# Up-projection with 512-column products on a joined activation tile, and an eviction in three stages

## The chip, the cores and the metric

The kernel runs on one core of one Trainium2 chip. The metric is the device time in microseconds of that core. Three runs of the kernel before took 1162.98, 1164.25 and 1164.31 us; their median is 1164.25 us. Engine names are those of the profile: PE is TensorE's matmul, PEld its weight load, DVE is VectorE, ACT is ScalarE, POOL is GpSimd, SP is SyncE.

## The reference

One layer of a decoder trunk on 256 tokens of width 2048: a mixing block (sparse attention beside a causal convolution) with its residual, then a gated MLP with a causal depthwise convolution of three taps, then a last norm. The change lies in the MLP, and there in the up-projection:

```python
def conv_glu_ffn(h, w_up, cw, cb, w_down):
    u = causal_depthwise_conv(h @ w_up, cw, cb)
    a, gate = jnp.split(u, 2, axis=-1)
    return (jax.nn.silu(gate) * a) @ w_down
...
    h = rms_norm(x, ffn_norm_g[l])
    x = x + conv_glu_ffn(h, w_up[l], ffn_conv_w[l], ffn_conv_b[l], w_down[l])
return rms_norm(x, final_norm_g)
```

`h` is 256 x 2048, `w_up` 2048 x 11264 (5632 columns for `a`, then 5632 for `gate`), `w_down` 5632 x 2048; all values are float32.

## The kernel before

**Numbers in two parts.** TensorE takes float32 operands here in the fp32r format, which keeps fewer bits. So each operand is held as a high part (the value rounded to fp32r) and a low part (what the rounding left). A product is made of three: high by high, high by low, low by high. `mm3` (L137 to L139) does this with the weights stationary: `wh` by `xt_h`, `wh` by `xt_l`, `wl` by `xt_h`, each 128 x 128 weights by 128 x 256 activations, added up in one PSUM bank. `mm_rows` (L144 to L146) does it with the activations stationary and 512 weight columns moving; the out-projection and the down-projection use it.

**Weights.** They come in chunks of 128 x 2048 floats (1 MB) in a fixed list, by DMA from SP's queue into one of three `wraw` buffers. `w_split` makes the high part on ScalarE (L109, `wh`) and the low part on VectorE (L114, `wl`, which needs `wh`); some chunks early in the kernel have their low part made on GpSimd. When the low part is done, the DMA of the chunk three places later is released. `w_next` hands chunk c to TensorE and, ahead of that, puts the split of chunk c + 2 into the queues of ScalarE and VectorE. There are three pairs of `wh` and `wl` buffers, so the high part of chunk c + 2 waits until TensorE has finished chunk c - 1.

**Order.** The schedule is manual: each engine does its instructions in the order in which the program issues them. The stages follow each other on TensorE: in-projection with attention and convolution woven in, out-projection, up-projection, down-projection, last norm.

**Up-projection.** The activations are transposed, in two tiles `xt_h` and `xt_l` of 128 x 16 x 256 (16 blocks of the contraction, 256 tokens); `norm_evac` (L177 on ScalarE, L178 on VectorE) fills them from the transposed residual. The norm's factor per token, `rB`, is not in them and is multiplied into the result. The loop has 22 rounds `m`, each with two passes `part` (0 for `a`, 1 for `gate`), each with two weight chunks `kh`. A pass makes two tiles of 128 features x 256 tokens, in the left halves of two PSUM banks, from 2 x 16 blocks of weights. The eight banks are used in turn by four passes. During the first pass the last transposes of the residual and the spreading of `rB` are put between the products (`between`).

After the products of a pass, its eviction is issued at once, one tile after the other. `conv3` multiplies the bank by `rB` into `u` on VectorE (L898), makes the third tap with its bias on ScalarE (`yt`, L900) and adds the other two taps on VectorE (L903 twice). In part 1, ScalarE then makes the silu (`sgf`, L935) and VectorE multiplies it with part 0's tile into `gt` (L936). All this stands in the queues of ScalarE and VectorE ahead of the next chunk's split.

**Down-projection.** `gsplit` splits four tiles of `gt` at a time into high and low (L892, L893), two groups ahead, eleven groups twice over. `down_chunk` then makes 512-column products into four banks.

Of the kernel before, what the change touches and what calls it, by code (L numbers as in the profile page):

```python
# [11 lines left out]
F32 = mybir.dt.float32  # L12
# [5 lines left out]
P = 128  # L18
# [28 lines left out]
def hybrid_trunk(ctx: ExitStack, tc: tile.TileContext, a: dict, out: bass.AP):  # L47
# [133 lines left out]
    x_rows = a["x"].rearrange("(t p) d -> p t d", p=P)  # L181

    mixp = ctx.enter_context(tc.tile_pool(name="mix", bufs=1))
    xt_h = mixp.tile([P, KD, T], F32R, name="xt_h")
    xt_l = mixp.tile([P, KD, T], F32R, name="xt_l")
    rB = mixp.tile([P, T], F32, name="rB")


# [683 lines left out]
    with ExitStack() as fx:  # L872
# [20 lines left out]
            nc.vector.tensor_sub(gl, src, gh.bitcast(F32))  # L893
            gq.append((gh, gl))

        def conv3(c, bank):
            u = fw.tile([P, T], F32, name="u", bufs=4)
            nc.vector.tensor_mul(u, bank[:, :T], rB)  # L898
            yt = fw.tile([P, T], F32, name="yt", bufs=6)
            nc.scalar.activation(yt, u, AF.Identity, scale=fcw[:, c, 2:3], bias=fcw[:, c, 3:4])  # L900
            for k in (1, 0):
                d = 2 - k
                nc.vector.scalar_tensor_tensor(yt[:, d:], u[:, :T - d], fcw[:, c, k:k + 1], yt[:, d:],  # L903
                                               op0=OP.mult, op1=OP.add)
            return yt


        for t in range(2):
# [5 lines left out]
        for m in range(NFT // 2):  # L914
            ya = {}
            if m == NFT // 2 - 1:
                gsplit()
            for part in range(2):
                bk = UP_BANKS[2 * ((2 * m + part) % 4):][:2]
                for kh in range(2):  # L920
                    wh, wl = [w.rearrange("p (k c) -> p k c", c=256) for w in w_next(1 if m + part + kh else 2)]
                    for n, (k, i) in enumerate((k, i) for k in range(8) for i in range(2)):
                        kt = kh * 8 + k
                        sl = slice(i * P, (i + 1) * P)
                        mm3(bk[i][:, :T], wh[:, k, sl], wl[:, k, sl], xt_h[:, kt], xt_l[:, kt],
                            kt == 0, kt == KD - 1)
                        if m + part == 0 and (kh, n) in between:
                            between.pop((kh, n))()
                for i in range(2):
                    yt = conv3(part * NFT + 2 * m + i, bk[i])  # L930
                    if part == 0:
                        ya[i] = yt
                    else:
                        sg = fw.tile([P, T], F32, name="sgf", bufs=2)
                        nc.scalar.activation(sg, yt, AF.Silu)  # L935
                        nc.vector.tensor_mul(gt[:, 2 * m + i], sg, ya[i])  # L936

        NQ = NFT // 4
        ss3 = fp.tile([P, 2, 5], F32, name="ss3")
# [43 lines left out]
        for h in range(2):  # L983
            prev, db = db, [(bank[2:] + bank[:2])[4 * h + 2 * t:][:2] for t in range(2)]
            for q in range(NQ):
                g = gq.pop(0)
                gsplit()
                if h == 1 and q == NQ - 1:
                    for t in range(2):
                        nc.vector.tensor_add(x2[:, t, 1536:], db[t][1], x2[:, t, 1536:])  # L990
                w0 = w_next()
                if prev and 0 < q < 5:
                    first_half(prev, (q - 1) // 2, (q - 1) % 2)
                if h == 1 and q == NQ - 1:
                    w1_ = w_next()
                    for t in range(2):
                        last_rows(w0, w1_, g, db[t], t)
                    break
                for t in range(2):
                    down_chunk(w0, g, db[t], 2 * q, t)  # L1000
                w1_ = w_next()
                for t in range(2):
                    down_chunk(w1_, g, db[t], 2 * q + 1, t)

# [87 lines left out]
```

## Time and profile before

| what | value |
|---|---|
| median of three runs | 1164.25 us |
| profiled execution: its own time | 1164.46 us |
| profiled execution: its span | 1162.7 us |
| PE, PEld, DVE, ACT busy, share of the span | 98%, 91%, 64%, 50% |
| mean granted TensorE clock | 0.993 |
| up-projection, first product to first product of the down-projection | 398.48 to 907.02 us |

A row of a group of instructions reads: line, engine, operation, written tile <- read tiles, sizes, count | busy us, mean ns of one | idle time of the engine just before them and what ended it. A row of the timeline reads: start in us from the span's start, duration in us, engine, line, operation. A row of the busy time in a stretch reads: the stretch, its length, then busy time of PE, PEld, DVE, ACT and POOL with the number of instructions, granted clock, DMA share, GB/s. Ends of matmuls are modelled and consecutive ones overlap, so a matmul's cost in a stream is the distance from one start to the next, not its duration. The weight load's row (PEld) lies beside the products.

### The profile page before, as it was taken

To read this page: it belongs to the slowest core of one execution; us is meant where nothing else is said; L and a number is where in the kernel's file an instruction comes from. 1 tells how busy PE (TensorE), PEld (TensorE's weight loads), DVE (VectorE), ACT (ScalarE), POOL (GpSimd) and SP (SyncE) were. 2 spreads that over 40 slices of the span, in tenths; PEclk is the share of its full clock that TensorE was granted. 3 is DMA by queue.
4 is the path that set the end of the run, shared out by engine and by line. 5 is a ranking of instruction groups with operands and counts; after the bars stand their busy time and mean duration, and the time that the engine had idled before them with its cause. 6 is when DMAs were issued, how large, how long until landed. Compare 5 with 4: busy or idle time off the path is not lost.

```text
span 1162.7 us, 18834 instructions
## 1 busy us (share of the span) xinstructions
PE 1136.0 (98%) x7890; PEld 1058.0 (91%) x7890; DVE 748.7 (64%) x1162; ACT 582.3 (50%) x810; POOL 128.2 (11%) x80
## 2 busy tenths in 40 slices
PE   8999999889899999999999999999999999999997
PEld 8999999888778899999999999999999888888886
DVE  6699569676455666667666666666666655556544
ACT  6534256788754544444535444544454444444443
POOL 1979553000000000000000000000000000000000
PEclk9999999999999999999999999999999999999998
DMA  9567416222264545545554545454545555555551
GB/s 367 194 240 260 152 53 252 73 79 94 70 265 152 211 169 194 204 160 183 181 215 147 198 174 209 145 215 171 196 149 210 191 182 203 185 185 181 182 180 73
DMA packets 32290, 207.62 MB, mean 179 GB/s; under 512 B 3867, under 2 KB 6187, under 8 KB 8012
## 3 DMA queue, kind: packets, MB, share of 16 engines
q1 hardware_dynamic: 28592, 199.64, 48.0%
q10 hardware_dynamic: 3612, 6.76, 1.6%
q8 instruction: 62, 1.02, 0.4%
q14 instruction: 24, 0.20, 0.1%
HBM read 204.27 MB, written 2.12 MB: 178 GB/s over the span
## 4 chain that ended last, share of the span: by engine, by line
PE 87%; ACT 5%; DVE 4%; DMA 2%; issue 1%; POOL 1%; DVEq 0%; POOLq 0%; ACTq 0%
PE bank L139 18%; PE bank L137 18%; PE bank L138 18%; PE bank L146 9%; PE bank L145 9%; PE bank L144 9%; DMA xr<-in_x 2%; ACT wh L109 1%; PE bank L437 1%; ACT e L643 1%; DVE wl L114 1%; PE bank L677 1%; ACT e L658 1%; PE bank L664 1%; POOL wl L114 0%
## 5 line engine op out<-in xcount | busy, mean ns | idle before, releaser
L137 PE MATMUL bank<-xt_h,wh 128*128 128x256 f32 x1920 | 546.9, 285 | 1.8 <-ACT wh L238 1.7
L139 PE MATMUL bank<-xt_h,wl 128*128 128x256 f32 x1920 | 544.8, 284 | 1.8 <-POOL wl L114 1.5
L138 PE MATMUL bank<-xt_l,wh 128*128 128x256 f32 x1920 | 544.5, 284 | 0.0
L114 DVE TENSOR_TENSOR wl<-wraw,wh 128x2048 fp32r<-128x2048 f32 (+1 forms) x185 | 360.6, 1967 | 126.9 <-ACT wh L109 126.8
L109 ACT ACTIVATE wh<-wraw 128x2048 fp32r<-128x2048 f32 (+2 forms) x239 | 352.7, 1501 | 135.7 <-PE bank L146 68.7
L137 PEld LDWEIGHTS bank<-xt_h,wh 128*128 128x128 f32 x1920 | 369.3, 192 | 3.9 <-ACT wh L238 2.5
L139 PEld LDWEIGHTS bank<-xt_h,wl 128*128 128x128 f32 x1920 | 369.3, 192 | 2.4 <-POOL wl L114 1.7
L138 PEld LDWEIGHTS bank<-xt_l,wh 128*128 128x128 f32 x1920 | 369.5, 192 | 0.7
L900 ACT ACTIVATE yt<-u,vecs 128x256 f32<-128x256 f32 x88 | 53.0, 603 | 204.0 <-DVE u L898 204.0
L144 PE MATMUL bank<-wh,gh 128*128 128x512 f32 (+1 forms) x360 | 140.8, 391 | 0.0
L146 PE MATMUL bank<-wh,gl 128*128 128x512 f32 (+1 forms) x360 | 140.8, 391 | 0.0
L145 PE MATMUL bank<-wl,gh 128*128 128x512 f32 (+1 forms) x360 | 140.8, 391 | 0.0
L903 DVE SCALAR_TENSOR_TENSOR yt<-u,vecs,yt 128x255 f32<-128x255 f32 (+1 forms) x176 | 85.1, 484 | 62.2 <-ACT yt L900 59.1
L114 POOL TENSOR_TENSOR wl<-wraw,wh 128x1024 fp32r<-128x1024 f32 (+1 forms) x54 | 120.7, 2271 | 36.1 <-ACT wh L109 36.1
L173 POOL TENSOR_TENSOR rstd<-ms,half 128x1 f32<-128x1 f32 x4 | 2.2, 549 | 876.0 <-DVE ms L166 876.0
L363 DVE SCALAR_TENSOR_TENSOR bank<-us,cw,bank 128x256 f32<-128x256 f32 x232 | 93.7, 483 | 4.2 <-ACT bank L358 3.7
L146 PEld LDWEIGHTS bank<-wh,gl 128*128 128x128 f32 x360 | 67.8, 188 | 15.8
L145 PEld LDWEIGHTS bank<-wl,gh 128*128 128x128 f32 x360 | 67.8, 188 | 15.8
L144 PEld LDWEIGHTS bank<-wh,gh 128*128 128x128 f32 x360 | 67.8, 188 | 15.8
L892 ACT ACTIVATE gh<-gt 128x1024 fp32r<-128x1024 f32 x22 | 23.3, 1059 | 64.6 <-PE bank L145 64.6
L898 DVE TENSOR_TENSOR u<-bank,rB 128x256 f32<-128x256 f32 x88 | 37.0, 420 | 26.3 <-PE bank L139 26.3
L893 DVE TENSOR_TENSOR gl<-gt,gh 128x1024 fp32r<-128x1024 f32 x22 | 27.0, 1225 | 41.0 <-ACT gh L892 41.0
(179 smaller groups left out, 860.4 us busy)
## 6 DMA issues: line engine op xcount, KB each, us to landing
wraw<-in_w_u SPq DMA_DIRECT2D x88, 1024.0 KB, 5.0
wraw<-in_w_d SPq DMA_DIRECT2D x44, 1024.0 KB, 4.9
wraw<-in_w_t SPq DMA_DIRECT2D x30, 1024.0 KB, 4.8
wraw<-in_w_o SPq DMA_DIRECT2D x16, 1024.0 KB, 4.9
wraw<-in_w_vg SPq DMA_DIRECT2D x4, 608.0 KB, 3.7
hb<-in_head SPq DMA_DIRECT2D x2, 1024.0 KB, 10.8
xr<-in_x SPq DMA_DIRECT2D x2, 1024.0 KB, 16.9
wb<-rel_scratch ACTq DMA_DIRECT2D x1, 2048.0 KB, 10.8
```

The costliest lines, as they stand in the source:

```text
L109: nc.scalar.activation(h[:, sl], raw[:, sl], AF.Copy)
L114: (nc.gpsimd if pooled else nc.vector).tensor_sub(l[:, sl], raw[:, sl], h[:, sl].bitcast(F32))
L137: nc.tensor.matmul(ps, wh, xh, start=first, stop=False)
L138: nc.tensor.matmul(ps, wh, xl, start=False, stop=False)
L139: nc.tensor.matmul(ps, wl, xh, start=False, stop=last)
L144: nc.tensor.matmul(ps, xh, wh, start=first, stop=False)
L145: nc.tensor.matmul(ps, xh, wl, start=False, stop=False)
L146: nc.tensor.matmul(ps, xl, wh, start=False, stop=last)
L363: nc.vector.scalar_tensor_tensor(y[:, j] if last else acc[0], us[:, j, k:k + T], cw[:, j, k:k + 1], acc[0], op0=OP.mult, op1=OP.add)
L898: nc.vector.tensor_mul(u, bank[:, :T], rB)
L900: nc.scalar.activation(yt, u, AF.Identity, scale=fcw[:, c, 2:3], bias=fcw[:, c, 3:4])
L903: nc.vector.scalar_tensor_tensor(yt[:, d:], u[:, :T - d], fcw[:, c, k:k + 1], yt[:, d:], op0=OP.mult, op1=OP.add)
```

## The change

`xt_h` and `xt_l` become the two halves of one tile `xt` (128 x 16 x 2 x 256), so that the high and low activations of a block of the contraction lie side by side. In the up-projection, `wh` meets both in one product of 512 columns (L957), which fills a whole bank: high by high in the left half, high by low in the right. `wl` by `xt_h` (L959) is added to the left half.

The eviction has to add the two halves. It is now three functions. `join` copies the right half to `u` on ScalarE (L907), adds the left half on VectorE (L908) and multiplies by `rB` (L909), for each of the two tiles. `three_taps` does what was L900 and L903 (now L916 and L920). `gate`, in part 1 alone, does the silu in place (L927) and the product into `gt` (L928). `up_stages` issues one stage of each pending pass per chunk, just after that chunk's split has been issued and ahead of its products; the last ones are issued in the first chunks of the down-projection. The tile `sgf` goes, `yt` has eight buffers instead of six.

```diff
-    xt_h = mixp.tile([P, KD, T], F32R, name="xt_h")
-    xt_l = mixp.tile([P, KD, T], F32R, name="xt_l")
+    xt = mixp.tile([P, KD, 2, T], F32R, name="xt")
+    xt_h, xt_l = xt[:, :, 0], xt[:, :, 1]
...
-        def conv3(c, bank):
-            u = fw.tile([P, T], F32, name="u", bufs=4)
-            nc.vector.tensor_mul(u, bank[:, :T], rB)
-            yt = fw.tile([P, T], F32, name="yt", bufs=6)
-            nc.scalar.activation(yt, u, AF.Identity, scale=fcw[:, c, 2:3], bias=fcw[:, c, 3:4])
-            for k in (1, 0):
-                d = 2 - k
-                nc.vector.scalar_tensor_tensor(yt[:, d:], u[:, :T - d], fcw[:, c, k:k + 1], yt[:, d:],
-                                               op0=OP.mult, op1=OP.add)
-            return yt
+        stages = []
+        def up_out(m, part, banks, ya):
+            us_, ys = [], []
+            def join():
+                for i in range(2):
+                    u = fw.tile([P, T], F32, name="u", bufs=4)
+                    nc.scalar.activation(u, banks[i][:, T:], AF.Copy)
+                    nc.vector.tensor_add(u, banks[i][:, :T], u)
+                    nc.vector.tensor_mul(u, u, rB)
+                    us_.append(u)
+            def three_taps():
+                for i in range(2):
+                    c = part * NFT + 2 * m + i
+                    yt = fw.tile([P, T], F32, name="yt", bufs=8)
+                    nc.scalar.activation(yt, us_[i], AF.Identity, scale=fcw[:, c, 2:3], bias=fcw[:, c, 3:4])
+                    ys.append(yt)
+                    for k in (1, 0):
+                        d = 2 - k
+                        nc.vector.scalar_tensor_tensor(ys[i][:, d:], us_[i][:, :T - d], fcw[:, c, k:k + 1],
+                                                       ys[i][:, d:], op0=OP.mult, op1=OP.add)
+                    if part == 0:
+                        ya[i] = ys[i]
+            def gate():
+                for i in range(2):
+                    nc.scalar.activation(ys[i], ys[i], AF.Silu)
+                    nc.vector.tensor_mul(gt[:, 2 * m + i], ys[i], ya[i])
+            stages.append([join, three_taps] + [gate] * part)
+        def up_stages():
+            for q in list(stages):
+                q.pop(0)()
+                if not q:
+                    stages.remove(q)
...
+                    up_stages()
                     for n, (k, i) in enumerate((k, i) for k in range(8) for i in range(2)):
                         kt = kh * 8 + k
                         sl = slice(i * P, (i + 1) * P)
-                        mm3(bk[i][:, :T], wh[:, k, sl], wl[:, k, sl], xt_h[:, kt], xt_l[:, kt],
-                            kt == 0, kt == KD - 1)
+                        nc.tensor.matmul(bk[i], wh[:, k, sl], xt[:, kt].rearrange("p a t -> p (a t)"),
+                                         start=kt == 0, stop=False)
+                        nc.tensor.matmul(bk[i][:, :T], wl[:, k, sl], xt_h[:, kt], start=False, stop=kt == KD - 1)
...
-                for i in range(2):
-                    yt = conv3(part * NFT + 2 * m + i, bk[i])
-                    if part == 0:
-                        ya[i] = yt
-                    else:
-                        sg = fw.tile([P, T], F32, name="sgf", bufs=2)
-                        nc.scalar.activation(sg, yt, AF.Silu)
-                        nc.vector.tensor_mul(gt[:, 2 * m + i], sg, ya[i])
+                up_out(m, part, bk, ya)
```

In the down-projection's loop, `up_stages()` is added after each of the two `w_next()` calls.

How the order of the instructions changes is shown at three places. The first is TensorE at the seam between two passes of the up-projection, in the kernel before; a number behind a tile's name tells buffers apart, and names in "waits" are the engines or DMA queues whose semaphore the instruction waits for.

```order
L137 MATMUL bank_68<-xt_h,wh 128x256
L138 MATMUL bank_68<-xt_l,wh 128x256
L139 MATMUL bank_68<-xt_h,wl 128x256
L137 MATMUL bank_69<-xt_h,wh 128x256
L138 MATMUL bank_69<-xt_l,wh 128x256
L139 MATMUL bank_69<-xt_h,wl 128x256
L137 MATMUL bank_70<-xt_h,wh 128x256 [waits Activation_49]
L138 MATMUL bank_70<-xt_l,wh 128x256
L139 MATMUL bank_70<-xt_h,wl 128x256 [waits DVE_49]
```

The same seam on TensorE in the changed kernel:

```order
L957 MATMUL bank_68<-xt,wh 128x512
L959 MATMUL bank_68<-xt,wl 128x256
L957 MATMUL bank_69<-xt,wh 128x512
L959 MATMUL bank_69<-xt,wl 128x256
L957 MATMUL bank_70<-xt,wh 128x512 [waits Activation_49]
L959 MATMUL bank_70<-xt,wl 128x256 [waits DVE_49]
```

Two instructions stand where three stood for a block, with the same two waits at the seam: for the high part of the weights and for the low one. In the whole program TensorE has 6245 rows instead of 7653, 1408 fewer.

The second place is VectorE in the middle of the up-projection, before: two splits, then the eviction of a gate pass, then the next splits.

```order
L114 TENSOR_TENSOR wl<-wraw,wh 128x2048 [waits DMAHW0_49,Activation_49]
L114 TENSOR_TENSOR wl<-wraw,wh 128x2048 [waits DMAHW1_49,PE_49,Activation_49]
L898 TENSOR_TENSOR u<-bank_64,rB 128x256 [waits PE_49]
L903 SCALAR_TENSOR_TENSOR yt<-u,vecs,yt 128x255 [waits Activation_49]
L903 SCALAR_TENSOR_TENSOR yt<-u,vecs,yt 128x254 [waits DVE_49]
L936 TENSOR_TENSOR gt<-sgf,yt 128x256 [waits Activation_49]
L898 TENSOR_TENSOR u<-bank_65,rB 128x256 [waits PE_49]
L903 SCALAR_TENSOR_TENSOR yt<-u,vecs,yt 128x255 [waits Activation_49]
L903 SCALAR_TENSOR_TENSOR yt<-u,vecs,yt 128x254 [waits DVE_49]
L936 TENSOR_TENSOR gt<-sgf,yt 128x256 [waits Activation_49]
L114 TENSOR_TENSOR wl<-wraw,wh 128x2048 [waits DMAHW2_49,Activation_49]
```

The same engine in the changed kernel, over a chunk with a gate and a join and the chunk after it with the taps:

```order
L114 TENSOR_TENSOR wl<-wraw,wh 128x2048 [waits DMAHW0_49,PE_49,Activation_49]
L928 TENSOR_TENSOR gt<-yt 128x256 [waits Activation_49] x2
L908 TENSOR_TENSOR u<-bank_70,u 128x256 [waits Activation_49]
L909 TENSOR_TENSOR u<-u,rB 128x256 [waits DVE_49]
L908 TENSOR_TENSOR u<-bank_71,u 128x256 [waits Activation_49]
L909 TENSOR_TENSOR u<-u,rB 128x256 [waits DVE_49]
L114 TENSOR_TENSOR wl<-wraw,wh 128x2048 [waits DMAHW1_49,PE_49,Activation_49]
L920 SCALAR_TENSOR_TENSOR yt<-u,vecs,yt 128x255 [waits Activation_49]
L920 SCALAR_TENSOR_TENSOR yt<-u,vecs,yt 128x254 [waits DVE_49]
L920 SCALAR_TENSOR_TENSOR yt<-u,vecs,yt 128x255 [waits Activation_49]
L920 SCALAR_TENSOR_TENSOR yt<-u,vecs,yt 128x254 [waits DVE_49]
```

Every chunk now has one split and behind it one or two stages; VectorE's first read of a bank waits for ScalarE's copy instead of for TensorE.

The third place is ScalarE at the same point, in the kernel before:

```order
L109 ACTIVATE wh<-wraw 128x2048 [waits DMAHW0_49,PE_49]
L109 ACTIVATE wh<-wraw 128x2048 [waits DMAHW1_49,PE_49,Activation_49]
L900 ACTIVATE yt<-u,vecs 128x256 [waits DVE_49]
L935 ACTIVATE sgf<-yt 128x256 [waits DVE_49,Activation_49]
L900 ACTIVATE yt<-u,vecs 128x256 [waits DVE_49]
L935 ACTIVATE sgf<-yt 128x256 [waits DVE_49,Activation_49]
```

And in the changed kernel, behind the same two splits:

```order
L109 ACTIVATE wh<-wraw 128x2048 [waits DMAHW0_49,PE_49,Activation_49]
L927 ACTIVATE yt<-yt 128x256 [waits DVE_49,Activation_49] x2
L907 ACTIVATE u<-bank_70 128x256
L907 ACTIVATE u<-bank_71 128x256 [waits PE_49]
L109 ACTIVATE wh<-wraw 128x2048 [waits DMAHW1_49,PE_49]
L916 ACTIVATE yt<-u,vecs 128x256 [waits DVE_49] x2
```

The silus of one pass and the copies of the next now stand behind the first of the two splits, the third taps behind the second.

More of the change, by code (lines that the diff above doesn't have):

```diff
@@ L991, in hybrid_trunk @@
                 w0 = w_next()
+                up_stages()
                 if prev and 0 < q < 5:
@@ L1001, in hybrid_trunk @@
                 w1_ = w_next()
+                up_stages()
                 for t in range(2):
```

## The prediction

> **What bounds the kernel now.** I read the page first, for the shares of the engines and for the chain that ended last.
>
> ```profile
> span 1162.7 us, 18834 instructions
> PE 1136.0 (98%) x7890; PEld 1058.0 (91%) x7890; DVE 748.7 (64%) x1162; ACT 582.3 (50%) x810; POOL 128.2 (11%) x80
> ...
> PE 87%; ACT 5%; DVE 4%; DMA 2%; issue 1%; POOL 1%; DVEq 0%; POOLq 0%; ACTq 0%
> ```
>
> TensorE (PE) carries 87% of the chain, so a faster side engine is worth nothing by itself. These shares are averages over stages, though, and the change touches one stage. Its bounds are in the timeline of TensorE (start us, duration, engine, line, operation): the first up-projection product, a steady stretch, and the seam to the down-projection.
>
> ```profile
> 398.48 0.28 PE L137 MATMUL bank<-xt_h,wh 128*128 128x256 f32 x1
> ...
> 412.02 0.28 PE L137 MATMUL bank<-xt_h,wh 128*128 128x256 f32 x1
> ...
> 906.66 0.28 PE L137 MATMUL bank<-xt_h,wh 128*128 128x256 f32 x1
> 906.78 0.28 PE L138 MATMUL bank<-xt_l,wh 128*128 128x256 f32 x1
> 906.90 0.28 PE L139 MATMUL bank<-xt_h,wl 128*128 128x256 f32 x1
> 907.02 0.39 PE L144 MATMUL bank<-wh,gh 128*128 128x512 f32 x1
> ```
>
> The stage lasts 907.02 - 398.48 = 508.54 us. I call the three products of one weight block (L137, L138, L139) a triple; there are 22 x 2 x 2 x 16 = 1408. The next two views, the busy time in the steady stretch and the groups of instructions in it, tell what a triple takes and what the other engines do meanwhile (columns of the groups: busy us, mean ns of one, idle before).
>
> ```profile
> 412.00:906.00 494.00, 494.00 (x4119) 494.00 (x4118) 327.81 (x386) 227.83 (x215) 0.00 (x0) 1.00 0.51 183
> ...
> L137 PE MATMUL bank<-xt_h,wh 128*128 128x256 f32 x1373 | 388.6, 283 | 0.0
> L114 DVE TENSOR_TENSOR wl<-wraw,wh 128x2048 fp32r<-128x2048 f32 x86 | 195.2, 2291 | 57.0 <-ACT wh L109 57.0
> L903 DVE SCALAR_TENSOR_TENSOR yt<-u,vecs,yt 128x255 f32<-128x255 f32 x86 | 41.6, 484 | 57.7 <-ACT yt L900 57.7
> L898 DVE TENSOR_TENSOR u<-bank,rB 128x256 f32<-128x256 f32 x85 | 35.7, 420 | 25.0 <-PE bank L139 25.0
> L936 DVE TENSOR_TENSOR gt<-sgf,yt 128x256 f32<-128x256 f32 x42 | 17.9, 426 | 22.9 <-ACT sgf L935 22.9
> L109 ACT ACTIVATE wh<-wraw 128x2048 fp32r<-128x2048 f32 x86 | 161.6, 1904 | 19.1 <-ACT wh L109 12.0 <-issue 4.5 <-PE bank L138 2.6
> L900 ACT ACTIVATE yt<-u,vecs 128x256 f32<-128x256 f32 x86 | 51.8, 602 | 199.1 <-DVE u L898 199.1
> L935 ACT ACTIVATE sgf<-yt 128x256 f32<-128x256 f32 x42 | 17.6, 418 | 47.5 <-DVE yt L903 47.5
> ```
>
> The first row reads: 494 us, PE busy all of it, PEld (weight loads) all of it, VectorE (DVE) 66%, ScalarE (ACT) 46%, granted clock 1.00, DMA 51%. TensorE waits for nobody: its groups show 0.0 idle. The group counts 1373 starts up to 906.00 and two more follow to 906.66, so from 412.02 there are 1374 distances: a triple takes 494.64 / 1374 = 0.360 us and a product of 256 columns 120 ns. The whole stage is 1408 x 0.360 = 506.9 us; the other 1.6 us lie at its start. The 283 ns in the group row is one product's latency; products overlap, and only the distance of starts counts. What the change is worth is therefore 1408 x (0.360 - the new distance from block to block), as long as the evictions stay hidden.
>
> **The products.** A block now has two products: 512 columns of wh on the pair xt_h, xt_l, and 256 columns of wl. Columns streamed are the same, 768; one weight load of three is gone. No row of before has this alternation in this stage, so I bound its two parts by the nearest rows. First the attention stage, where 256 and 512 columns stand in turn, and then the down-projection (512) and the last rows of the kernel (256).
>
> ```profile
> 255.09 0.28 PE L623 MATMUL bank<-k_l,qs 128*128 128x256 f32 x1
> 255.21 0.39 PE L622 MATMUL bank<-k_h,qs 128*128 128x512 f32 x1
> 255.44 0.39 PE L623 MATMUL bank<-k_l,qs 128*128 128x512 f32 x1
> 255.67 0.28 PE L137 MATMUL bank<-xt_h,wh 128*128 128x256 f32 x1
> ```
>
> ```profile
> 1049.70 0.39 PE L144 MATMUL bank<-wh,gh 128*128 128x512 f32 x1
> 1049.93 0.40 PE L145 MATMUL bank<-wl,gh 128*128 128x512 f32 x1
> ...
> 1055.32 0.39 PE L144 MATMUL bank<-wh,gh 128*128 128x512 f32 x1
> ...
> 1145.99 0.28 PE L144 MATMUL bank<-wh,gh 128*128 128x256 f32 x1
> ...
> 1146.69 0.28 PE L144 MATMUL bank<-wh,gh 128*128 128x256 f32 x1
> ```
>
> In attention a 256 followed by a 512 takes 0.12 us, and two 512s take 255.67 - 255.21 = 0.46, 230 ns each, the last of them followed by a 256. In the down-projection 24 products of 512 (every third is an L144) take 1055.32 - 1049.70 = 5.62 us, 234 ns each. At the end six products of 256 take 0.70 us, 117 ns each. So 512 columns cost 230 to 234 and 256 columns 117 to 120 where TensorE waits for nothing. The block takes 347 to 354 ns instead of 360. For the 256 I take 120, the row with the same operands; for the 512 the middle, 232, since attention has the alternation and the down-projection the weight traffic (rows of equal weight). That is 352 ns: **1408 x 8 ns = 11.3 us gained.** With the ends it is 8.4 us (354) and 18.3 us (347). Beyond them, single starts such as 1050.87 to 1051.11 below lie 240 apart; were that the mean, nothing would be left.
>
> ```profile
> 1050.87 0.40 PE L146 MATMUL bank<-wh,gl 128*128 128x512 f32 x1
> 1051.11 0.40 PE L144 MATMUL bank<-wh,gh 128*128 128x512 f32 x1
> ```
>
> The Trainium skill's page "TensorE: Matmul & The Clock Gate", section "Back-to-back issue gap", puts a warm product at N / 2.4 + 2.5 ns. By it three products of 256 would take 327.5 and the new pair 325, a gain of 1408 x 2.5 ns = 3.5 us. The trace disagrees with both levels: 120 against 109 at 256 columns, 230 to 234 against 216 at 512.
>
> **The removed weight load.** The loads show whether it was in the way. The rows are those of TensorE's loads (PEld) beside its products.
>
> ```profile
> 600.06 0.28 PE L138 MATMUL bank<-xt_l,wh 128*128 128x256 f32 x1
> 600.07 0.19 PEld L139 LDWEIGHTS bank<-xt_h,wl 128*128 128x128 f32 x1
> 600.18 0.28 PE L139 MATMUL bank<-xt_h,wl 128*128 128x256 f32 x1
> ```
>
> Each load starts 0.01 us after the product before it and runs beside it. It is not added to the 120 ns, so I do not count 1408 loads as saved; only the measured distances of starts count.
>
> **The evictions.** Per output tile the old path is L898, L900, two L903 (and L935, L936 in the second part). The new one adds a ScalarE copy of the bank's upper half and a VectorE add (L908), and moves the rB product to SBUF (L909). The nearest rows for the copy are a copy of 384 columns out of PSUM and a scaled one of 256.
>
> ```profile
> L669 ACT ACTIVATE es<-bank x32: 469/491/494, 210.4 to 314.0; 128x384 f32<-128x384 f32 x32
> ...
> L177 ACT ACTIVATE xt_h<-bank,vecs x16: 454/470/482, 369.9 to 404.7; 128x256 fp32r<-128x256 f32 x16
> ```
>
> I take 0.47 us, no more than 0.60 (L900); the add is like L898, 0.42, and the product in SBUF like L936, 0.43. One round of m (two passes of two weight chunks each, 64 blocks) lasts 64 x 0.352 = 22.5 us. VectorE needs in it 4 x 2.29 + 4 x (0.42 + 0.43) + 8 x 0.484 + 2 x 0.426 = 17.3 us, 77%; ScalarE 4 x 1.90 + 4 x 0.47 + 4 x 0.60 + 2 x 0.42 = 12.7 us, 57%. Both stay under the round. Their cost on the path is therefore nothing, hidden by the products; no gain comes from them either, since TensorE never waited for them.
>
> The order matters more than the sum. The new add waits for ScalarE's copy, which stands behind that chunk's wh (L109). Queued behind the add on VectorE are the rB product and the next chunk's wl (L114); TensorE waits for that wl. The longest chunk is the one with gate and join: wh 1.90, wl 2.29, two gate products 0.85, two adds and two products 1.70, together 6.7 us against 16 x 0.352 = 5.63 for the chunk. It runs 1.1 us into the next chunk, but VectorE would there first wait 1.90 us for the next wh. The wl that the chunk itself makes is for the chunk after the next: ready 4.2 us after the start, needed at 11.3. The cover is 7 us.
>
> The bank is read by the join 4 us after its pass ends and is written again three passes of 11.3 us later, so TensorE gains no wait there. SP's queue is not moved past anything: the DMA of a raw chunk is still released by wl, and the evictions stand behind it.
>
> ```profile
> wraw<-in_w_u SPq DMA_DIRECT2D x88, 1024.0 KB, 5.0
> ```
>
> A chunk lands in 5.0 us and there are three raw buffers, so chunks every 5.63 us instead of 5.76 cost nothing; the DMA share goes from 0.51 to about 0.52. At the stage's end join, taps and gate of the last pass move behind the first three weight chunks of the down-projection. They fill gt 40 to 43, which only the last of eleven groups reads, ten groups of 11.2 us later: nothing. At its start the first product of a block now needs xt_l too, which L178 writes 16 blocks ahead: nothing.
>
> **The sum.** 1164.46 us (the profiled execution, span 1162.7) - 11.3 = 1153.2. That execution lies 0.2 above the median of the runs, 1164.25, which gives 1153.0. A measurement of this kernel can tell some 0.2% from no change, 2.3 us.
>
> **Rivals.**
> A, only columns count: 768 columns at 120 per 256 remain 360 ns, the removed load was hidden and nothing is won: 1164.25. For it speaks that loads run beside products; against it, that 512 columns take 230 to 234 and not 240 in two stages. Everything from 356 ns a block upwards (6 us gained or less) is counted here. By the page of the Trainium skill named above, the saving of one fixed 2.5 ns a block would give 1160.7, which is in this case. Chance 0.11, of which 0.06 lie within 2.3 us.
> B, both parts at their short ends: with the longer product in front the 256 falls to the 117 of the kernel's end, and the 512 to attention's 230: 347 ns, 1164.25 - 18.3 = 1145.9. Against it: 117 was seen only where the weight traffic had ended. Chance 0.10.
> C, slower: ScalarE, waiting in its queue for a VectorE result (L916 for the rB product, L927 for the taps), starts the next wh only after VectorE's evictions are done. Then wh, wl and evictions are one chain per chunk: with the gate 6.7, join alone 5.9, taps twice 6.1, in all 24.9 us against 22.5, so 22 x 2.35 = 52 us lost, 1205. It decides when VectorE ends more than 7 us into the next chunk; I count 1.1. Chance 0.03.
> D, the change doesn't do what it says: if xt were no run of 512 columns the product would not be one instruction. The program has 1408 TensorE rows fewer, so I leave it at 0.
>
> **How the numbers follow.** The forecast, a block between 348 and 356 ns, has 0.75; with A 0.11, B 0.10, C 0.03, a hundredth is left for the unforeseen. Its own range is 1147 to 1159. For 8 in 10 I reach to B's price and a little into A: 1145 to 1160; left out are C and the weaker part of A, and what lies below B. Faster 0.91, same 0.06, slower 0.03.
>
> **What would show it.** In the new profile the up-projection would last about 497 us from first to last product. L957 to L959 would lie 0.23 apart and L959 to L957 0.12; 0.24 and 0.12 would make A right. TensorE would still be without idle time from 412 us on, and VectorE near 77%. Any wait of TensorE for L109 or L114 there would make the eviction part wrong. Outside the stage nothing should move.

## The result, and the profile after

| | before | after |
|---|---|---|
| median (range) of 4 runs each, us | 1164.28 (1162.98 to 1165.78) | 1145.95 (1143.48 to 1148.03) |
| profiled execution: own time / span, us | 1164.46 / 1162.7 | 1145.46 / 1143.3 |
| up-projection, first product to first product of the down-projection, us | 508.54 | 489.89 |
| from there to the end of the span, us (rounded) | 255.6 | 255.6 |
| mean distance from block to block, ns | 360.0 | 346.7 |

The changed kernel takes 0.9841 of the time before (95% interval 0.9818 to 0.9865): 18.3 us less. The prediction said 11.3 us less, 1153.0, with a range of 1145 to 1160. So the sign and the place were right, and one term was too small. The median lies in the stated range by 0.95 us only, and below the forecast's own range of 1147 to 1159.

The page of the kernel after, the same rows as were read of the page before:

```profile
span 1143.3 us, 16193 instructions
PE 1116.6 (98%) x6482; PEld 977.6 (86%) x6482; DVE 767.7 (67%) x1250; ACT 598.3 (52%) x898; POOL 128.3 (11%) x80
...
PE 87%; ACT 5%; DVE 4%; DMA 2%; issue 1%; POOL 1%; DVEq 0%; POOLq 0%; ACTq 0%
```

The shares look as before: TensorE is busy for 98% of the span and 87% of the chain. A shorter span with the same shares is what a kernel shows whose bounding engine simply got less to do. Only the column PEld fell, from 91 to 86%. The timeline of TensorE of the same kernel has the bounds of the stage and a steady stretch:

```profile
397.80 0.39 PE L957 MATMUL bank<-xt,wh 128*128 128x512 f32 x1
...
702.22 0.39 PE L957 MATMUL bank<-xt,wh 128*128 128x512 f32 x1
702.45 0.27 PE L959 MATMUL bank<-xt,wl 128*128 128x256 f32 x1
...
702.92 0.39 PE L957 MATMUL bank<-xt,wh 128*128 128x512 f32 x1
...
887.69 0.39 PE L144 MATMUL bank<-wh,gh 128*128 128x512 f32 x1
```

The stage lasts 887.69 - 397.80 = 489.89 us, 18.65 less than before. Everything behind it is as long as it was, and its start differs by 0.68 us, less than it scatters in runs in which nothing ahead of it was changed (396.0 to 400.4 us). Two blocks take 702.92 - 702.22 = 0.70 us. Between 412 and 880 us the distance from L957 to L959 is 231.7 ns in the mean and from L959 to L957 115.0 ns: 346.7 instead of the 352 that I had taken, and 1408 x 13.3 ns = 18.7 us instead of 11.3.

Then what the other engines do in the steady stretch: the row of the windows, the groups of instructions, and all the waits that this stretch has (columns: waited us, times, longest).

```profile
412.00:880.00 468.00, 468.00 (x2702) 409.27 (x2701) 346.05 (x462) 239.92 (x298) 0.00 (x0) 1.00 0.54 191
```

```profile
L957 PE MATMUL bank<-xt,wh 128*128 128x512 f32 x1351 | 468.4, 393 | 0.0
...
L957 PEld LDWEIGHTS bank<-xt,wh 128*128 128x128 f32 x1351 | 253.3, 187 | 58.8
...
L916 ACT ACTIVATE yt<-u,vecs 128x256 f32<-128x256 f32 x84 | 45.2, 586 | 0.0
...
L908 DVE TENSOR_TENSOR u<-bank,u 128x256 f32<-128x256 f32 x84 | 35.1, 418 | 0.0
L907 ACT ACTIVATE u<-bank 128x256 f32<-128x256 f32 x86 | 27.4, 369 | 0.0
```

```profile
ACT wh L109 <- issue: 124.4, 43, 3.1
DVE wl L114 <- ACT wh L109: 117.6, 85, 2.2
ACT wh L109 <- PE bank L957: 105.4, 42, 3.1
```

TensorE is busy for all of the 468 us and waits for nobody: no row of the waits begins with PE. VectorE is at 346.05 / 468 = 74% (forecast 77%) and ScalarE at 51% (57%), in part since the copy out of PSUM takes 369 ns and not the 470 that I took from the nearest row. For 105.4 us ScalarE waits for TensorE to release a weight buffer, so the side engines run ahead of the products, not behind them. (For another 124.4 us it stands ahead of L109 without a cause that the profile names.) PEld was busy without a gap before; now 58.8 us of idle time stand ahead of the loads for L957, 1351 times 43.5 ns: the load ahead of each, for L959, takes 188 ns beside a 512-column product that stands 231.7 ns from the next.

### The profile page after: what moved, and what is told of

It reads as the page before. It is cut to its first block, busy times and chain, and to the rows that moved or that the text cites. A ratio compares the mean times of both kernels' runs of the same rounds, so it can differ in the third digit from the quotient of the medians.

```text
span 1143.3 us, 16193 instructions
## 1 busy us (share of the span) xinstructions
PE 1116.6 (98%) x6482; PEld 977.6 (86%) x6482; DVE 767.7 (67%) x1250; ACT 598.3 (52%) x898; POOL 128.3 (11%) x80
## 4 chain that ended last, share of the span: by engine, by line
PE 87%; ACT 5%; DVE 4%; DMA 2%; issue 1%; POOL 1%; DVEq 0%; POOLq 0%; ACTq 0%
PE bank L957 28%; PE bank L959 14%; PE bank L145 9%; PE bank L144 9%; PE bank L146 9%; PE bank L139 4%; PE bank L137 4%; PE bank L138 4%; DMA xr<-in_x 2%; ACT wh L109 1%; PE bank L437 1%; ACT e L643 1%; DVE wl L114 1%; PE bank L677 1%; ACT e L658 1%
## 5 line engine op out<-in xcount | busy, mean ns | idle before, releaser
L109 ACT ACTIVATE wh<-wraw 128x2048 fp32r<-128x2048 f32 (+2 forms) x239 | 355.9, 1505 | 356.5 <-issue 149.6
L957 PE MATMUL bank<-xt,wh 128*128 128x512 f32 x1408 | 488.6, 394 | 0.0
L959 PE MATMUL bank<-xt,wl 128*128 128x256 f32 x1408 | 390.0, 277 | 0.0
L957 PEld LDWEIGHTS bank<-xt,wh 128*128 128x128 f32 x1408 | 264.0, 188 | 61.1
L959 PEld LDWEIGHTS bank<-xt,wl 128*128 128x128 f32 x1408 | 264.4, 188 | 0.0
L137 PE MATMUL bank<-xt,wh 128*128 128x256 f32 x512 | 147.8, 289 | 1.7 <-ACT wh L238 1.7
L139 PE MATMUL bank<-xt,wl 128*128 128x256 f32 x512 | 146.3, 286 | 1.9 <-POOL wl L114 1.6
L138 PE MATMUL bank<-xt,wh 128*128 128x256 f32 x512 | 146.1, 285 | 0.0
L137 PEld LDWEIGHTS bank<-xt,wh 128*128 128x128 f32 x512 | 99.0, 193 | 3.5 <-ACT wh L238 2.1
L139 PEld LDWEIGHTS bank<-xt,wl 128*128 128x128 f32 x512 | 99.0, 193 | 2.5 <-POOL wl L114 1.8
L138 PEld LDWEIGHTS bank<-xt,wh 128*128 128x128 f32 x512 | 99.0, 193 | 0.6
L920 DVE SCALAR_TENSOR_TENSOR yt<-u,vecs,yt 128x255 f32<-128x255 f32 (+1 forms) x176 | 80.9, 481 | 3.1
```

What stands on the lines that cost most here:

```text
L109: nc.scalar.activation(h[:, sl], raw[:, sl], AF.Copy)
L137: nc.tensor.matmul(ps, wh, xh, start=first, stop=False)
L138: nc.tensor.matmul(ps, wh, xl, start=False, stop=False)
L139: nc.tensor.matmul(ps, wl, xh, start=False, stop=last)
L920: nc.vector.scalar_tensor_tensor(ys[i][:, d:], us_[i][:, :T - d], fcw[:, c, k:k + 1], ys[i][:, d:], op0=OP.mult, op1=OP.add)
L957: nc.tensor.matmul(bk[i], wh[:, k, sl], xt[:, kt].rearrange("p a t -> p (a t)"), start=kt == 0, stop=False)
```

## The experiments

The questions: is the gain TensorE's alone, and why is it 13.3 ns a block and not 8? And is the eviction in stages a condition of it, or could it have stayed as it was?

**1. The old three products in the changed kernel.** Layout, banks with two halves and staged eviction stay, only the product of 512 columns is cut in two again.

```diff
-matmul(bk[i], wh, xt[:, kt])
+matmul(bk[i][:, :T], wh, xt_h[:, kt])
+matmul(bk[i][:, T:], wh, xt_l[:, kt])
 matmul(bk[i][:, :T], wl, xt_h[:, kt])
```

> The changed kernel, but each block again has three products of 256 columns: wh by xt_h into the left half, wh by xt_l into the right half, wl by xt_h into the left half. Layout and three-stage eviction stay. Theory L (what costs is the third weight load: loads with only 256 columns between them come no faster than one in 120 ns): starts 120 ns apart, 360 a block, the whole gain gone, 1164 us, within 1.5. Rival C (the 256-column product became cheaper, 115 ns, by the joined tile, the halves of the bank or the other eviction): 345 to 350 a block, 1144 to 1150 us.

Measured: 1164.91 us (10 runs), ratio to before 1.0009 (0.9999 to 1.0018). The timeline of TensorE in this kernel:

```profile
700.07 0.28 PE L957 MATMUL bank<-xt,wh 128*128 128x256 f32 x1
700.19 0.28 PE L959 MATMUL bank<-xt,wh 128*128 128x256 f32 x1
700.31 0.28 PE L961 MATMUL bank<-xt,wl 128*128 128x256 f32 x1
700.43 0.28 PE L957 MATMUL bank<-xt,wh 128*128 128x256 f32 x1
```

Three starts 0.12 us apart, a block of 360 ns, and the stage at 508.53 us: the time before, to 0.01 us of the stage. So neither the layout of xt nor the staged eviction is worth anything by itself, and the gain needs the longer product. It also says that the 115 ns of the short product are no property of its operands: the same product on the same operands, in the same place and the same bank, stands at 120 here.

**2. Two products of 512.** The low weights meet the pair as well. This adds the low-by-low part, which both kernels leave out, and it measures what a 512 costs in this very stage.

```diff
-matmul(bk[i][:, :T], wl, xt_h[:, kt])
+matmul(bk[i], wl, xt[:, kt])
```

> The changed kernel, but wl too meets both halves in 512 columns (the small low-by-low product is added as well). Two loads and 1024 columns a block. Theory L with 512 columns at the distance that the changed kernel shows (232 ns): 464 a block, 1408 x 117 ns = 165 us more, 1311 us. Rival (a fixed 13.1 ns a load and 0.4176 ns a column, which the kernel before with 3 loads and 768 columns and the changed one with 2 loads and 768 columns give together): 454 a block, 1297 us. With the 234.3 of the down-projection it is 468.6 a block, 1317 us.

Measured: 1293.65 us (one run). The timeline of TensorE:

```profile
699.72 0.39 PE L959 MATMUL bank<-xt,wl 128*128 128x512 f32 x1
...
701.08 0.39 PE L959 MATMUL bank<-xt,wl 128*128 128x512 f32 x1
```

Six distances in 1.36 us, 227 ns each (226.7 over the stage), so the block is 453.4 ns and not 464. My reading that a 512 costs 232 ns falls. What holds is a sum of two parts, solved from 120.0 at 256 columns and 226.7 at 512: 106.7 ns for 256 further columns, 0.4167 ns a column, and 13.3 ns for each product with its weight load. It gives the changed kernel's block as well, which was not used in solving it: 226.7 + 120.0 = 346.7, measured 346.7. The 231.7 and 115.0 of the single distances are this sum divided in another way. The change takes one product and one load of three away from each block, and that is worth 13.3 ns.

Two sizes always give a constant and a slope, so a third size is needed as a test. The kernel before has one, which I had overlooked: 96 products of 304 columns in a row, ahead of the attention. The first and the last:

```profile
177.17 0.30 PE L531 MATMUL bank<-wh,xt_h 128*128 128x304 f32 x1
...
190.42 0.30 PE L533 MATMUL bank<-wh,xt_l 128*128 128x304 f32 x1
```

The 95 distances are 139.5 ns in the mean; 13.3 ns and 304 columns at 0.4167 give 140.0.

The Trainium skill's page "TensorE: Matmul & The Clock Gate", section "Back-to-back issue gap", has the same form for a single product's gap, N / 2.4 + 2.5 ns. The slope agrees: 1 / 2.4 is 0.4167. The constant does not: 13.3 measured against 2.5. By an estimate with the page's 2.5, the whole change would have been worth 1408 x 2.5 ns = 3.5 us instead of 18.7.

**3. Products in pairs.** Both 512s of two blocks first, then both 256s: does it matter that the products alternate?

```diff
 matmul(bk[i], wh, xt[:, kt])
-matmul(bk[i][:, :T], wl, xt_h[:, kt])
+for j in range(2 * i):                      # both, behind the second 512
+    matmul(bk[j][:, :T], wl[:, k, j * P:(j + 1) * P], xt_h[:, kt])
```

> The changed kernel with the products of two blocks reordered: 512, 512, 256, 256 columns instead of 512, 256, 512, 256. Same loads, same columns. Theory L (a load is ready early only if a 512-column product runs before the one that it belongs to): the first 256 stays at 115 ns, the second goes to 120, so 5 ns more in 704 pairs, 3.5 us, 1149.5 us. Rival C (a 256-column product costs 115 wherever it stands): 1146 us and both at 115.

Measured: 1147.43 us (4 runs), ratio to before 0.9842 (0.9828 to 0.9857). Between 412 and 880 us the four distances are 233.4, 114.6, 115.8 and 232.9 ns in the mean: 696.7 for two blocks against 693.3 alternating. The stage is 2.5 us longer. I had thought that the 256 is short because its load is ready early behind a long product; then the second 256, behind a short one, should have stood at 120. It stands at 115 or 116, so that falls. It also shows how far the sum of experiment 2 carries: here it misses by 3.4 ns in 697.

**4. Without the weight traffic.** The prediction had tied the 117 ns of the kernel's last rows to weight traffic that had ended. In the kernel before, 85 of the 88 weight chunks of the up-projection are neither loaded nor split, and the third chunk's weights are used in their place, so this kernel leaves out what the other weights would compute.

```diff
+chunks[up0 + 3:up0 + 2 * NFT] = [None] * (2 * NFT - 3)   # no DMA
...
+if chunks[c] is None: parts[c] = kept[0]; return        # no split
```

> The kernel before, with the weight traffic of the up-projection left out: only its first three chunks are loaded and split, the other 85 use the third one's weights, so the output is not the reference's. TensorE has the same products. Theory (a product with its weight load costs 13.3 ns and 0.4167 ns a column, whatever moves in memory beside it): starts stay 120 ns apart, 360 a block, 1164 us. Rival (the 117 ns of the kernel's last 256-column products come from the end of the weight traffic): 117, 351 a block, 1152 us.

Measured: 1164.07 us (one run), starts 120.0 ns apart, the stage 508.53 us. The DMA share from 412 to 880 us is 0.00 instead of 0.51. Traffic and splits take nothing from TensorE here, and the 120 is TensorE's own. Why the last rows stand at 117.3 stays open.

**5. The new products with the eviction at once.** Right behind a pass, per output tile, in the order of the kernel before: copy, add, rB product, third tap, two taps, gate. This is the other corner of the change.

```diff
-stages.append([join, three_taps] + [gate] * part)
+for i in range(2):      # behind the pass, no stages
+    nc.scalar.activation(u, banks[i][:, T:], AF.Copy)
+    nc.vector.tensor_add(u, banks[i][:, :T], u)
+    nc.vector.tensor_mul(u, u, rB)
+    nc.scalar.activation(yt, u, AF.Identity, ...)      # then two taps on VectorE
+    ...                                                # with a gate: Silu, tensor_mul
```

> The changed kernel with its 512-column products, but each pass's eviction is issued in one piece behind its products, one tile after the other, as in the kernel before (copy, add, rB, third tap, two taps, silu, gate). Theory (the evictions are hidden in either order, cover 7 us): TensorE stays without idle time in the stage, 346.9 ns a block, 1146 us, within 1.5. Rival (the staging is what makes the products' gain reachable: with the eviction ahead of the next split, weights come late): TensorE waits for L109 or L114 at the passes, 1 to 2 us in each of 44, 1190 us or more.

Measured: 1162.69 us (10 runs), ratio to before 0.9983 (0.9972 to 0.9995). Nearly the whole gain is gone. I had expected it hidden in either order, and that falls. The waits of this kernel between 412 and 880 us, and its busy times there:

```profile
ACT yt L909 <- DVE u L907: 155.0, 82, 3.3
DVE yt L912 <- ACT yt L909: 55.0, 82, 0.7
...
DVE wl L114 <- ACT wh L109: 44.5, 41, 1.4
ACT u L905 <- PE bank L947: 30.7, 22, 3.1
...
PEld bank L947 <- DVE wl L114: 9.6, 19, 0.8
PE bank L947 <- DVE wl L114: 1.9, 4, 0.5
DVE u L906 <- ACT u L905: 1.2, 2, 0.8
```

```profile
412.00:880.00 468.00, 464.46 (x2615) 399.63 (x2614) 339.94 (x449) 238.71 (x286) 0.00 (x0) 1.00 0.49 183
```

VectorE is at 73% and ScalarE at 51%, no more than in the changed kernel, and yet TensorE waits for wl. The rows of the waits say why: ScalarE waits for VectorE (L909 for L907) and VectorE for ScalarE (L912 for L909), tile by tile, so that both are idle in turn. The timelines of ScalarE and of VectorE over one eviction:

```profile
705.61 3.71 ACT L109 ACTIVATE wh<-wraw 128x2048 fp32r<-128x2048 f32 x2
709.22 0.39 ACT L905 ACTIVATE u<-bank 128x256 f32<-128x256 f32 x1
712.87 0.60 ACT L909 ACTIVATE yt<-u,vecs 128x256 f32<-128x256 f32 x1 [3.26 <-DVE u L907]
713.38 0.36 ACT L905 ACTIVATE u<-bank 128x256 f32<-128x256 f32 x1
715.33 0.60 ACT L909 ACTIVATE yt<-u,vecs 128x256 f32<-128x256 f32 x1 [1.60 <-DVE u L907]
715.84 3.70 ACT L109 ACTIVATE wh<-wraw 128x2048 fp32r<-128x2048 f32 x2
```

```profile
707.54 4.50 DVE L114 TENSOR_TENSOR wl<-wraw,wh 128x2048 fp32r<-128x2048 f32 x2 [1.39 <-ACT wh L109]
711.95 0.42 DVE L906 TENSOR_TENSOR u<-bank,u 128x256 f32<-128x256 f32 x1
712.41 0.42 DVE L907 TENSOR_TENSOR u<-u,rB 128x256 f32<-128x256 f32 x1
...
717.77 4.50 DVE L114 TENSOR_TENSOR wl<-wraw,wh 128x2048 fp32r<-128x2048 f32 x2 [0.80 <-ACT wh L109]
```

ScalarE's L909 stands ahead of the next two wh in its queue and waits 3.26 us, first for VectorE's two splits and then for its add and product. The next wh start at 715.84, when the second L909 is out, and VectorE, done with the taps, waits for them. The two queues are one chain. ScalarE's copy does wait for TensorE (L905 for L947, 22 times), but VectorE waited for that copy only twice (L906 for L905), both times before TensorE's first wait, so that TensorE isn't part of the chain. One round of it takes 22.99 us (the distance of TensorE's waits); the products of a round need 64 x 0.3467 = 22.2 us, and 22 x 0.8 us are the 17 us that are missing.

The rows of PE show only 3.5 us of idle time in the 468, because the wait is not all that fills the 0.8 us: most rounds of this kernel also have their blocks 353.3 ns apart instead of 346.7. That pace is not what sets the round. These are the first products behind three waits in turn:

```profile
480.24 0.40 PE L945 MATMUL bank<-xt,wh 128*128 128x512 f32 x1
...
503.23 0.40 PE L945 MATMUL bank<-xt,wh 128*128 128x512 f32 x1
...
526.22 0.39 PE L945 MATMUL bank<-xt,wh 128*128 128x512 f32 x1
```

The blocks of the first of the two rounds are 353.3 ns apart and those of the second 346.8, and both rounds last 22.99 us: the faster products only wait longer at their end, 0.79 us instead of 0.38.

In the kernel before, the round was 64 x 0.360 = 23.04 us, and its chain, shorter by the copy and the add, had room in it. Its waits over the same stretch show that:

```profile
ACT yt L900 <- DVE u L898: 190.1, 82, 4.0
...
DVE u L898 <- PE bank L139: 24.0, 20, 1.2
```

The first row is the same to and fro; the second is the room, 1.2 us in each of 20 rounds in which VectorE waited for TensorE.

**6. The eviction in one piece, behind the split.** As experiment 5, but called where the stages are called, behind the split in the next pass's first chunk. Is it enough that the eviction stands behind the split, or must it be cut?

```diff
-stages.append([join, three_taps] + [gate] * part)
+stages.append([all_of_it])      # the body of experiment 5
```

> The changed kernel with each pass's eviction behind the next chunk's split, as changed, but in one piece and one tile after the other instead of in three stages. Theory (what the change needs is the cut into stages: in one piece ScalarE and VectorE wait for each other inside the eviction, some 6.8 us from the first add to the last gate, and ScalarE's next wh stands behind its last silu): the two engines' chain sets the round, about 23.4 us instead of 22.2, with TensorE waiting for L109 or L114, 22 x 1.2 = 26 us more, 1172 us. Rival (it is enough that the eviction stands behind the split): 1146 us, TensorE without idle time.

Measured: 1162.25 us (10 runs), ratio to before 0.9985 (0.9974 to 0.9996). The waits between 412 and 880 us:

```profile
ACT yt L910 <- DVE u L908: 186.3, 81, 3.3
...
PEld bank L950 <- DVE wl L114: 9.1, 17, 0.8
```

The same picture and the same round, 23.0 us, as without the shift. What removes the chain is the cut: with a chunk between the stages, ScalarE finds each stage's input ready. In the changed kernel L916 stands at 0.0 idle; here L910, the same instruction, was waited for 186.3 us. My round of 23.4 us (1172) was a little too long. One thing is not separated: the stages also take the two tiles of a pass together, where the piece takes one after the other, and no run has the one without the other.

**7. More work in the join.** The changed kernel with two more VectorE products of 256 columns per output tile, whose results nobody reads: is there really a cover?

```diff
 nc.vector.tensor_mul(u, u, rB)
+for _ in range(2):
+    nc.vector.tensor_mul(idle, u, rB)
```

> The changed kernel with two more VectorE products of 128 x 256 per tile in the join, to nobody's use: 3.4 us more on VectorE in each round of 22.2 us, 20.7 us in all. Theory (the three stages leave a cover of some 7 us): TensorE without idle time, 1146 us, within 1.5. Rival (the staged chain has as little room as the chain of the eviction at once, which sets a round of 22.99 us): the 3.4 us a round come through, 22 x 2.6 us or more, 1200 us.

Measured: 1144.09 us (4 runs), ratio to before 0.9823 (0.9807 to 0.9839), the stage again 489.89 us. The row of the windows of this kernel:

```profile
412.00:880.00 468.00, 468.00 (x2701) 409.28 (x2700) 414.14 (x630) 240.17 (x298) 0.00 (x0) 1.00 0.53 191
```

VectorE at 414.14 / 468 = 88%, and TensorE still busy throughout. 3.4 us more per round cost nothing. Beside experiments 5 and 6, where VectorE at 73% delays TensorE, this is the clearest sign that the order decides and not the load.

**8. One moving operand for two products in a row, in the down-projection.** The 234 ns there had misled me. One thing that differs from the up-projection: there the two products of a block share xt_h as moving operand, here the moving operand changes with every product. The order was turned so that both token halves meet the same weights in turn.

```diff
+for x, w in ((0, 0), (1, 0), (0, 1)):
+    for t in range(2):
+        matmul(banks[t][n], g[x][:, kt % 4, half t], ws[w][:, c])
```

> The changed kernel with the down-projection's products in another order: the two token halves innermost, so that four products in turn have the same moving operand, then two (before: each product another one). Same products, same loads. Theory M (512 columns cost 234.3 there and 226.7 in the run with two 512-column products a block because the moving operand changes with each product): 226.7 ns, 1032 x 7.6 ns = 7.8 us less, 1138 us. Rival (it is the stage, not the order): 234.3, 1146 us.

Measured: 1144.28 us (4 runs), ratio to before 0.9827 (0.9812 to 0.9841); the distances in the down-projection stay at 234.3 ns. The moving operand is not the reason.

**9. The same change in the input projection.** 22 of its weight tiles, each of 16 blocks with three products of 256, get the pair, with one copy and one add per tile.

```diff
-mm3(ps, wh[:, sl], wl[:, sl], xt_h[:, kt], xt_l[:, kt], ...)
+matmul(full, wh[:, sl], xt[:, kt])
+matmul(ps, wl[:, sl], xt_h[:, kt])
 ...
+nc.scalar.activation(half_r, full[:, T:], AF.Copy)
+nc.vector.tensor_add(ps, ps, half_r)
```

> The changed kernel, with the same edit in 22 chunks of the in-projection (gates and values from the second pair on, and the eight key and value tiles): wh meets both halves in 512 columns, ScalarE copies the right half, VectorE adds it. Theory (13.3 ns a product saved, the adds hidden): 22 x 16 x 13.3 ns = 4.7 us less, 1141.3 us. Rival (VectorE is near its limit in this stage, 22 x 0.42 us = 9.2 us of adds come onto the path): 1150 us.

Measured: 1152.83 us (4 runs), ratio to before 0.9899 (0.9885 to 0.9914), so some 7 us slower than the change alone. The up-projection begins at 405.7 us instead of 397.8. From the groups and from TensorE's waits, up to 400 us:

```profile
L354 DVE TENSOR_TENSOR bank<-bank,half_r 128x256 f32<-128x256 f32 x22 | 9.5, 430 | 24.5 <-ACT half_r L353 24.4
```

```profile
PE bank L676 <- ACT e L670: 9.9, 1, 9.9
```

Here TensorE isn't the only bound. The adds take 9.5 us on VectorE, which waits 24.4 us for the copies ahead of them. A single new wait of TensorE in the attention takes 9.9 us, more than the products can give: 22 tiles of 16 blocks, 13.3 ns each, are 4.7 us. That the adds and copies make that wait is argued from the rows, not shown by a run of its own.

**10. TensorE stopped once a round.** In experiment 5 the blocks were 346.7 ns apart until the first wait, and mostly 353.3 behind it. So the changed kernel got a stop: a small product that reads what ScalarE has just copied from the bank finished last, 20 times.

```diff
+nc.scalar.activation(tiny, last[1][:, :2], AF.Copy)
 wh, wl = w_next(...)
+nc.tensor.matmul(bk[0][:, :2], ident, tiny, start=True, stop=True)
```

> The changed kernel, with TensorE made to stop at the start of the rounds from the third on: a small product (128 x 2 columns) that waits for a ScalarE copy of two columns of the bank just finished. 20 stops, 0.3 to 1 us each. Theory (TensorE's pace is set by where it restarts after a wait, which would explain that the run with the eviction at once has blocks 353.3 ns apart after its first wait and 346.7 before): some rounds between stops at 353 instead of 346.7. Rival (the slower pace belongs to that run's eviction): all blocks between stops at 346.7, and only the stops themselves are lost, 6 to 20 us.

Measured: 1162.23 us (one run). The timeline of TensorE: a stop, the stretch ahead of it, which the stop before it had restarted, and a later stretch.

```profile
452.23 0.40 PE L962 MATMUL bank<-xt,wh 128*128 128x512 f32 x1
...
453.29 0.40 PE L962 MATMUL bank<-xt,wh 128*128 128x512 f32 x1
...
470.32 0.38 PE L957 MATMUL bank<-tiny,ident 128*128 128x2 f32 x2 [0.26 <-ACT tiny L954]
470.57 0.49 PE L962 MATMUL bank<-xt,wh 128*128 128x512 f32 x1
...
567.71 0.39 PE L962 MATMUL bank<-xt,wh 128*128 128x512 f32 x1
...
569.10 0.39 PE L962 MATMUL bank<-xt,wh 128*128 128x512 f32 x1
```

Three blocks take 1.06 us in the first stretch, 353 ns each, and four take 1.39 us in the last, 347 or 348 each. The first two stops were followed by the slower pace, all others by the faster. A stop makes the distance from its block to the next 0.67 us longer, and the one behind it 0.09 us. So the pace of identical products can change at a restart; what sets it stays open. In this run the down-projection, whose products nobody touched, stands at 232.4 ns instead of 234.3.

## Why the prediction was right, and where it was off

- **What bounds the stage: right.** TensorE waits for nobody, and a shorter block shortens the kernel one for one: 18.65 us in the stage, 18.3 in the medians, nothing behind the stage. Experiment 1 shows the other side, no gain without fewer products.
- **The old block, 360 ns as three times 120: right**, and it is TensorE's own (experiment 4).
- **The new block: mis-sized.** The step "for the 512 the middle, 232", with 120 for the 256, made 352; 346.7 was measured, so the term of 11.3 us should have been 18.7. The 232 came from attention (230 by the two distances shown, 233.3 in its longer sequences of 512 between 300 and 400 us) and from the down-projection (234), and the 120 from this stage: numbers of stages with different paces were added. In this stage a 512 takes 226.7 (experiment 2), a size for which the stage had no row before. What I could have done is to treat the product as a constant and a slope: the rows of 304 columns at 139.5 and of 256 at 120.0 give 0.406 ns a column, hence 224 for the 512 and 344 for the block, nearer than 352. With the slope of the Trainium skill's page "TensorE: Matmul & The Clock Gate", section "Back-to-back issue gap" (N / 2.4, so 0.4167 ns a column), the row of 120 ns leaves 120 - 106.7 = 13.3 for the constant, and that estimate comes out at 346.7. I compared the page's level with the trace and put it aside whole, slope included.
- **The range: luck in part.** The forecast of a block of 348 to 356 ns, which had 0.75, and its own range of 1147 to 1159 both missed. That 1145.95 lies within 1145 to 1160 is owed to the stretch down to Rival B's price and not to the working of the forecast; one of the four runs, 1143.48, lies below.
- **Rival B had the price, 347 ns and 1145.9, but not the reason.** It needed 230 and 117; the parts are 226.7 and 120. That ended weight traffic makes a 256 shorter is not borne out by experiment 4: without the traffic it stood at 120 in this stage.
- **Rival A** (the removed product and load are hidden) falls with experiments 1 and 2: each product with its load costs 13.3 ns beyond its columns. That a load runs beside a product does not make the product free. Whether the 13.3 ns belong to the load or to the product stays open, since in every kernel here each product has its own.
- **The evictions: right for the changed kernel.** No wait of TensorE, 74% and 51% against 77% and 57%; experiment 7 confirms the cover. But I weighed their order for the changed kernel alone. **Not priced** was that without the cut into stages they would have taken the gain back. I quoted the row of L900, 199.1 us of waiting for VectorE, and read it only as idle time off the path, not as a chain with a length of its own. A chain of ScalarE and VectorE such as Rival C's is real where the eviction is in one piece (experiments 5 and 6), with a round of 23.0 us; in the staged order, for which I worked out 24.9, none shows. The change has two halves, and each is worth next to nothing alone (the kernel before has no copy and no add to do):

| median, us | three products | two products |
|---|---|---|
| eviction at once | 1164.28 (before) | 1162.69 |
| eviction in stages | 1164.91 | 1145.95 (after) |

- **Banks, queues, the ends of the stage: right.** No such wait shows, and 255.6 us follow in both kernels.

None of the kernels tried beats the changed one by more than the runs scatter.

## What to carry to other kernels

Work out a product's time as a constant and a slope from rows of the same stage: here 13.3 ns for each product with its load and 0.4167 ns a column, so fewer and longer products pay even where the columns stay the same, as long as TensorE is the only bound (in experiment 9 it was not). Before the bounding engine is made faster, look how long one round of the side engines' chain takes, not how busy they are: 73% with mutual waits held TensorE up, 88% without them did not. Where ScalarE and VectorE pass a tile to and fro in queues that also feed TensorE, put one chunk of other work between the steps, as the stages here do.

## What the runs showed of the hardware

- Identical sequences of products run at one of two paces, 346.7 or 353.3 ns a block at a granted clock of 1.00, and the pace can change when TensorE has stood still (experiments 5 and 10). Without a stop it held: 1381 blocks of the changed kernel in a row are 346.7 ns apart in the mean.
- Products of 512 columns stood 226.7 ns apart in one stage and 234.3 in another of the same kind of kernel; leaving out the traffic of weights changed nothing for products of 256 (experiment 4), and another order of the moving operands changed nothing in the 234.3 (experiment 8), so the cause stays open.
- Single distances of starts mislead where shapes alternate: 231.7 and 115.0 ns are 226.7 and 120.0 in pure sequences, and only the sum is the same.
